# Attention scores in 128 rows, the last MLP pair in plain products, and the last key products in whole fp32, in a two-layer decoder segment

## The chip, the core and the metric

One NeuronCore of a Trainium2 chip runs the whole program in one launch. The metric is the device time of one execution in microseconds, the median of three runs: 1142.87 us (1142.51 to 1142.96) before the change. The engines are TensorE (PE: matrix products and transposes; PEld is its weight load), VectorE (DVE), ScalarE (ACT), GpSimd (POOL) and SyncE (SP, which issues most DMAs). The work of each engine is a list that it goes through in order.

## The reference, cut to what matters

Two layers, each of a mixer (sparse attention, retention, RWKV-7, short convolution), a cross-attention into 256 memory tokens and a squared-ReLU MLP, on 256 tokens of width 1024, all in fp32. The three places that the change touches:

```python
# mixer A: scores of the selected and the windowed branch, 4 heads of 64, here over all 256 keys
s = einsum('bqhd,bkd->bhqk', qb, k) * scale + bias          # then mask, softmax, times values
# cross-attention: keys of the memory tokens, one product per layer
k, v = jnp.split(rms_norm(mem, ln_mem[l]) @ xa_wkv[l], 2, axis=-1)
# MLP, and the norm at the layer's end
h = rms_norm(x, ln_mlp_pre[l])
x = x + rms_norm(jnp.square(jax.nn.relu(h @ mlp_w1[l])) @ mlp_w2[l], ln_mlp_post[l])
# the next layer begins with h = rms_norm(x, ln_mix_pre[l + 1])
```

## The kernel before, in words

**Precision.** A fast product reads fp32r operands. For full precision each operand is split in two fp32r parts, `hi` (ACT copies) and `lo` (DVE subtracts: `split`), and a product becomes three matmuls (`mm3`): hi·hi, hi·lo, lo·hi. A product of unsplit fp32 operands is one `mm`, which the chip's records show as two passes. Tokens stand in two blocks of 128 (`t`), so there are two of each row-wise step.

**Weights** come in units of 128x1024 numbers. `unit_order` lists them; `unit` brings one by DMA into a `raw` tile and splits it into a `hi` and a `lo` tile. `ftile` multiplies a unit of eight 128x128 blocks with the split, transposed activations: 8 x 3 matmuls of 256 columns.

**Order.** All operations are recorded first; `Sched` then deals them out to the engines' lists by estimated start times, with `rank` to break ties (lower goes first). `NB` gives the number of buffers of each tag. Tag `g8` (8 KB in each partition) has 7: each pair of split activations takes 2, and so does each pair of W2 sums in the MLP. PSUM has 8 banks, named by use: A, B, C and S.

**Attention scores** (`nsa_proj`, `nsa_pair`). The queries of two heads lie in rows 0-63 and 64-127 of one tile; the keys are stored twice, once in each half. A score tile is one `mm3` over the 64 rows of its head: 64x256 and 64x512 numbers moving, by token block; 8 such per layer, 16 in all.

**MLP** (`mlp`, `wpair`). Step j of 16: `up(j)` makes two units of W1 products (48 matmuls into one C bank), ReLU and square. `down(j)` multiplies with a pair of W2 units. It uses the seven-product form of a 2x2 block product: `factors` makes seven left sums, `wpair` four right operands and three right sums (the sums `u` and `w` in `g8`; part of it by an accumulating POOL DMA), and the seven `mm3` go into seven S banks, which stay open until j = 15. In layer 0 the order is up(0), then up(j) and down(j-1); in layer 1 up(j) and down(j-2). After the last products `comb` adds banks up to the four output blocks, and `post_bank` and `post` do the norm of a token block: a square with a sum on ACT, two small POOL operations (a scale-and-add and a power) and two DVE updates of `x` (tiles x_65 and x_67 for the blocks).

**Between the layers** `boundary` calls `post` and then `pre`: again squares on ACT and three POOL operations for the next norm, then DVE makes x·rstd·g, PE transposes it (8 per block, to C banks, `to_hT_half`), and ACT and DVE split the result into the next layer's activations. PE meanwhile works on `kpairs(1, (2, 3))`: four of the eight key units of layer 1 (B banks), held back for this place by `s.after`.

**Helpers.** Every record carries the line of its helper: L622 ACT operations, L633 DVE and POOL tensor_tensor, L639 scalar_tensor_tensor, L645 tensor_scalar, L667 the POOL power, L676 matmuls, L681 transposes, L716 DMAs of SP. In the changed kernel these lines are one lower. Numbers at the ends of tile names count the allocations.

Of the kernel before, what the change touches and what calls it, by code (L numbers as in the profile page):

```python
# [20 lines left out]
T = 256  # L21
# [3 lines left out]
C = 64  # L25
# [61 lines left out]
def unit_order():  # L87

    o = []
    for l in range(DEPTH):  # L90
        def add(lay, *names):
            o.extend((lay, n) for n in names)

        add(l, *[("rwkv", i) for i in RWKV_ORDER])
        add(l, ("nq", 0), ("nq", 1), ("kcvc", 0), ("kskw", 0))
        add(l, *[("tok%d" % g, k0) for g in (1, 2) for k0, _ in NT_CHUNKS])
        add(l, *[("ret", i) for i in range(4)])
        add(l, *[("conv", i) for i in range(6)])
        for m in Z_ORDER:
            for c in range(2):  # L100
                add(l, *[("z", m, c, k0) for k0 in range(0, 8, 2)])
                add(l, ("br", m, c))
        add(l, *[("mo", k) for k in range(8)])
        xv = [[("xv", c, k0) for k0 in range(0, 8, 2)] for c in range(2)]
        if l == 0:
            add(l, *[("xk", k) for k in range(8)])
        else:
            add(l, *xv[0])
        add(l, *[("xq", k) for k in range(8)])
        if l == 0:  # L110
            add(l, *xv[0])
        add(l, *xv[1])
        add(l, *[("xo", k) for k in range(8)])
        if l == 0:
            add(1, *[("xk", k) for k in range(4)])
        add(l, *[("w1", i) if l == 0 else ("w1t", 2 * i) for i in range(4 - 2 * (l == 0))])
        lag = 1 if l == 0 else 2
        for j in range(lag, 16 + lag):
            if j < 16:
                add(l, ("w1", 2 * j), ("w1", 2 * j + 1))  # L120
            add(l, ("w2", j - lag, 0), ("w2", j - lag, 1))
        if l == 0:
            add(1, *[("xk", k) for k in range(4, 8)])
    return o
# [105 lines left out]
NPS = {"A": 4, "B": 2, "C": 2, "S": 7}  # L230
# [367 lines left out]
class Prog:  # L598
# [332 lines left out]
    def pre(self, t, g, hT, normed, out):  # L931
# [11 lines left out]

        if normed:
            rstd = stat()
            for s in H2:
                self.stt(xg[:, s], x[:, s], rstd, g[:, s], OP.mult, OP.mult)
        else:
            for s in H2:
                self.tt(xg[:, s], x[:, s], g[:, s], OP.mult)  # L950
        for q in range(2):
            self.to_hT_half(t, q, xg[:, 512 * q:512 * q + 512], hT)
# [432 lines left out]
    def nsa_proj(self, l, hT):  # L1385
# [6 lines left out]
        q2 = pair()  # L1392
        self.split(*q2, q)
# [17 lines left out]
        self.nsap = q, L, q2, k2  # L1411
# [265 lines left out]
    def mem_prep(self, l):  # L1677
# [12 lines left out]
        mh, ml = self.new_hT()  # L1690
        for i in range(0, 8, 2):
            m = self.tile([128, 2, T], "g2")
# [13 lines left out]
    def kpairs(self, l, pairs, spill=None):  # L1706
        for i in pairs:
            p = self.bank("B", (128, 2, T))
            for j in range(2):
                self.ftile(l, ("xk", 2 * i + j), self.mhl, p[:, j])  # L1710
# [21 lines left out]
    def xattn(self, l):  # L1732
# [66 lines left out]
        if l == 0:  # L1799
            self.at(5, self.mem_prep, 1)  # L1800
# [64 lines left out]
    def mlp(self, l):  # L1865
        hT, rstd = self.hT, self.rs
        left = {}

        def factors(j, put):
# [3 lines left out]
            if a is not put:  # L1873
                put(a)
# [10 lines left out]
        def up(j):  # L1885
# [38 lines left out]
        if l == 0:  # L1924
            up(0)
        else:
# [12 lines left out]
        lag = 1 if l == 0 else 2  # L1939
        for j in range(lag, 14 + lag):  # L1940
            if j < 16:
                up(j)
            down((j - lag,), (1, 3, 2, 5, 7, 6, 4))
        if l == 0:
            up(15)
# [7 lines left out]
        down((14,), (1, 2, 6, 5, 3))  # L1953
        down((15,), (1, 2, 6, 5, 3))
        down((14, 15), (7, 4))
        self.lastdown = self.s.mains[-1]
# [3 lines left out]
        def end(t):  # L1960
            if last:
                self.post(t, st[t], rstd[t], out=orr[:, t])
            else:
                self.at(0, self.boundary, t, st[t], rstd[t], gpre, outT, True, self.rs)
# [8 lines left out]
        old = self.rank(0)  # L1973
# [4 lines left out]
        u4 = comb(u2, bank[5], OP.add)  # L1978
        comb(bank[3], u4, OP.subtract, 0, 1)
        end(0)  # L1980
        u3 = comb(u2, bank[7], OP.add)
        comb(u3, bank[5], OP.add, 1, 1)
# [6 lines left out]
    def run(self):  # L1989
# [5 lines left out]
        for l in range(DEPTH):  # L1995
# [72 lines left out]
```

## Time and profile before

| what | value |
|---|---|
| median of 3 runs | 1142.87 us |
| the profiled execution: its time, its span | 1143.17 us, 1141.4 us |
| mean granted TensorE clock | 0.994 |
| read from HBM, written | 223.48 MB, 3.15 MB |
| matmul records on PE | 7380 |

The span is from the first to the last instruction; 1.77 us of the execution lie around it. Windows and timelines count from the span's start. The mixer of layer 0 lies at 10 to about 290 us, its cross-attention up to about 400, its MLP up to 577, the change of layers at 577 to 600, and layer 1 follows in the same way, with its MLP from about 960 to 1130. A record's duration runs to the modelled end of the result; matmuls overlap, so what a matmul costs in a dense stretch is the distance from one start to the next.

### The profile page before, as it was taken

The numbers are of one execution on the slowest core, as the hardware profiler recorded it, in microseconds if no ns is written. First come the engines' busy times: TensorE is split into PE (matmuls) and PEld (weight loads), VectorE is DVE, ScalarE is ACT, GpSimd is POOL, SyncE is SP. The second block draws the span as 40 slices with busy tenths as digits, with TensorE's granted clock in tenths as the row PEclk, the third lists the DMA queues.
The fourth block names the chain that finished last, engine by engine and source line by source line (L and its number), as shares of the span: only waits on it lengthen the run. The fifth ranks groups of instructions, "written<-read, shape, count | busy, mean of one in ns | idle before, by whom it ended". The sixth has DMA issues, their size and how long they took to land. (4 is left out here: it accounts for less than half of the span.)

```text
span 1141.4 us, 19231 instructions
## 1 busy us (share of the span) xinstructions
PE 1113.1 (98%) x7380; PEld 977.0 (86%) x7380; DVE 868.9 (76%) x1332; ACT 662.6 (58%) x1055; POOL 105.3 (9%) x165
## 2 busy tenths in 40 slices
PE   8999999999999999999979999999999999999996
PEld 7898878788998899999869899888888986999994
DVE  5867785675857689989896678766857667998897
ACT  7545544544645567677674546454547455776673
POOL 3002000100200110000021002000002002000011
PEclk9999999999999999999999999999999999999998
DMA  8327456754537599999853155456655467899991
GB/s 323 119 89 242 128 155 194 251 193 148 184 131 240 181 271 277 289 278 257 281 188 106 32 194 171 148 168 192 223 192 167 141 213 211 242 271 280 261 267 52
DMA packets 76831, 226.83 MB, mean 199 GB/s; under 512 B 12319, under 2 KB 14111, under 8 KB 76612
## 3 DMA queue, kind: packets, MB, share of 16 engines
q1 hardware_dynamic: 72132, 208.83, 54.8%
q0 software_dynamic: 4608, 16.78, 8.5%
q8 instruction: 58, 0.95, 0.3%
q14 instruction: 33, 0.27, 0.1%
HBM read 223.48 MB, written 3.15 MB: 199 GB/s over the span
## 5 line engine op out<-in xcount | busy, mean ns | idle before, releaser
L633 DVE TENSOR_TENSOR lo<-raw,hi 128x1024 fp32r<-128x1024 f32 (+2 forms) x310 | 370.1, 1213 | 95.7 <-ACT hi L622 67.5
L622 ACT ACTIVATE hi<-raw 128x1024 fp32r<-128x1024 f32 (+2 forms) x310 | 317.7, 1049 | 139.8 <-PE A L676 83.6
L676 PE MATMUL A<-hi,g 128*128 128x512 f32 (+2 forms) x1152 | 368.1, 391 | 0.8 <-ACT g L622 0.5
L676 PEld LDWEIGHTS A<-hi,g 128*128 128x128 f32 x1152 | 215.0, 188 | 47.6 <-issue 2.2
L676 PE MATMUL A<-lo,g 128*128 128x512 f32 (+2 forms) x576 | 221.4, 384 | 0.0
L633 DVE TENSOR_TENSOR g<-g,g 128x512 f32<-128x512 f32 (+3 forms) x228 | 196.8, 891 | 5.7 <-ACT g L622 4.5
L622 ACT ACTIVATE g<-g 128x512 fp32r<-128x512 f32 (+7 forms) x232 | 155.2, 706 | 62.7 <-DVE g L633 41.2
L676 PE MATMUL A<-g,hi 128*128 128x256 f32 x928 | 179.3, 292 | 1.2 <-DVE g L633 1.2
L676 PE MATMUL C<-g,hi 128*128 128x256 f32 x960 | 172.0, 281 | 0.0
L676 PEld LDWEIGHTS A<-g,hi 128*128 128x128 f32 x928 | 145.1, 191 | 9.6 <-issue 6.3
L676 PEld LDWEIGHTS C<-g,hi 128*128 128x128 f32 x960 | 149.4, 189 | 2.4
L676 PE MATMUL C<-g,lo 128*128 128x256 f32 x480 | 135.1, 281 | 0.0
L676 PE MATMUL A<-g,lo 128*128 128x256 f32 x464 | 131.5, 283 | 0.4 <-DVE lo L633 0.4
L622 ACT ACTIVATE g<-C 128x512 fp32r<-128x512 f32 (+5 forms) x119 | 59.7, 515 | 117.2 <-PE C L676 80.5
L676 PEld LDWEIGHTS A<-lo,g 128*128 128x128 f32 x576 | 108.5, 188 | 20.9 <-issue 0.5
L676 PE MATMUL S<-g,g 128*128 128x512 f32 x480 | 117.1, 394 | 0.0
L676 PEld LDWEIGHTS S<-g,g 128*128 128x128 f32 x480 | 90.1, 188 | 21.0
L676 PEld LDWEIGHTS C<-g,lo 128*128 128x128 f32 x480 | 90.5, 189 | 0.0
L676 PEld LDWEIGHTS A<-g,lo 128*128 128x128 f32 x464 | 88.6, 191 | 0.6 <-DVE lo L633 0.6
L622 ACT ACTIVATE g<-A 128x512 f32<-128x512 f32 (+2 forms) x66 | 37.3, 566 | 54.1 <-PE A L676 51.3
L676 PE MATMUL B<-g,g 64*64 64x64 f32 (+4 forms) x896 | 67.8, 253 | 0.0
L676 PEld LDWEIGHTS B<-g,g 64*64 64x64 f32 (+2 forms) x896 | 59.0, 151 | 6.0 <-issue 2.1
(142 smaller groups left out, 1079.7 us busy)
## 6 DMA issues: line engine op xcount, KB each, us to landing
raw<-wts SPq DMA_DIRECT2D x298, 512.0 KB, 4.6
g<-wts SPq DMA_DIRECT2D x96, 256.0 KB, 5.7
g<-wts POOLq DMA_DIRECT2D x32, 512.0 KB, 6.5
g<-rows SPq DMA_DIRECT2D x11, 512.0 KB, 4.4
g<-memT SPq DMA_DIRECT2D x12, 256.0 KB, 5.9
g<-cmpw SPq DMA_DIRECT2D x4, 512.0 KB, 4.7
raw<-wts SPq DMA_DIRECT2D x4, 498.0 KB, 3.6
raw<-wts SPq DMA_DIRECT2D x4, 480.0 KB, 6.8
```

The costliest lines, as they stand in the source:

```text
L622: e = lambda: self.nc.scalar.activation(real(out), real(in_), func, bias=real(bias), scale=real(scale), accum_out=real(accum))
L633: f = lambda: e.tensor_tensor(real(out), real(a), real(b), op)
L676: e = lambda: self.nc.tensor.matmul(real(out), real(lhsT), real(rhs), start=start, stop=stop, skip_group_check=True)
```

## The change

1. **Scores in 128 rows.** `nsa_proj` now keeps the split queries of one head in one tile `qs`, `hi` in rows 0-63 and `lo` in rows 64-127. A score is two matmuls over 128 rows, with the `hi` and with the `lo` keys, which stand in both halves already. (The sum now has lo·lo as well.)
2. **Close of the MLP, both layers.** Step 15 no longer uses the seven-product form: `whole` and `plain` multiply its four left and right blocks as eight plain `mm3`. Banks 1, 5, 6 and 7 are complete after step 14, and their sums are put ahead at rank -1.5; a bank 8 is opened late. Layer 0 takes the order of layer 1 (down two steps behind up).
3. **Norm between the layers.** `pre` computes x·g at once; the factor rstd enters by the product that transposes, with a scaled identity, in fp32 instead of the transpose.
4. **Last key products.** The four key units held back multiply the unsplit weights with an unsplit, normalised memory tile `mraw` (a `g8` tile that lives from the cross-attention of layer 0 to here), as eight fp32 products each.

```diff
-        add(l, *[("w1", i) if l == 0 else ("w1t", 2 * i) for i in range(4 - 2 * (l == 0))])
-        lag = 1 if l == 0 else 2
-        for j in range(lag, 16 + lag):
+        add(l, *[("w1", i) if l == 0 else ("w1t", 2 * i) for i in range(4)])
+        for j in range(2, 18):
...
-            add(l, ("w2", j - lag, 0), ("w2", j - lag, 1))
+            add(l, ("w2", j - 2, 0), ("w2", j - 2, 1))
...
-    def to_hT_half(self, t, q, src, hT):
+    def to_hT_half(self, t, q, src, hT, scale=None):
...
-            self.tr(p[:, j], src[:, j * 128:(j + 1) * 128])
+            if scale is None:
+                self.tr(p[:, j], src[:, j * 128:(j + 1) * 128])
+            else:
+                self.mm(p[:, j], src[:, j * 128:(j + 1) * 128], scale)
...
+        for s in H2:
+            self.tt(xg[:, s], x[:, s], g[:, s], OP.mult)
+        scale = None
         if normed:
-            rstd = stat()
-            for s in H2:
-                self.stt(xg[:, s], x[:, s], rstd, g[:, s], OP.mult, OP.mult)
...
+            scale = self.tile([128, 128], "g1")
+            self.ts(scale, self.ident, stat())
...
-        q2 = pair()
-        self.split(*q2, q)
+        qs = self.tile([128, 2, 2, T], "g4", F32R)
+        for s in range(2):
+            self.split(qs[0:64, :, s], qs[64:128, :, s], p[64 * s:64 * s + 64])
...
-                self.mm3(p, *[v[po, a, t * 128:t * 128 + 128] for v in q], *[v[po, :, :nk] for v in k], True, True)
+                qt = q[:, a, h % 2, t * 128:t * 128 + 128]
+                with self.together():
+                    self.mm(p, qt, k[0][:, :, :nk], True, False)
+                    self.mm(p, qt, k[1][:, :, :nk], False, True)
...
+    def ftile_whole(self, l, name, moving, dst):
...
+        raw = self.tile([128, UNIT], "raw")
+        d = self.dma(raw, self.wts[i], lead=False)
...
+                for k in (k0, k0 + 1):
+                    self.mm(dst, raw[:, k * 128:(k + 1) * 128], moving[:, k, :], k == 0, k == 7)
...
-                    self.mm3(bank[n], *left[j][n], *right[j][n], j == 0, j == 15)
+                    self.mm3(bank[n], *left[j][n], *right[j][n], j == 0, j == 14 and n not in (2, 3, 4))
...
+        down((14,), (1, 6, 5, 7, 2, 3, 4))
+        old = self.rank(-1.5)
         self.act(p1, bank[1])
-        comb(p1, bank[2], OP.add, 0, 0)
         u2 = comb(p1, bank[6], OP.add)
         u4 = comb(u2, bank[5], OP.add)
+        u3 = comb(u2, bank[7], OP.add)
+        u5 = comb(u3, bank[5], OP.add)
+        self.rank(old)
+        bank[8] = self.bank("S")
+        us = [self.unit(l, ("w2", 15, h)) for h in range(2)]
...
+        plain(2, (0, 0, 0), (1, 1, 0))
+        plain(3, (0, 1, 1), (1, 0, 1))
+        self.rank(-1.5)
+        comb(p1, bank[2], OP.add, 0, 0)
         comb(bank[3], u4, OP.subtract, 0, 1)
         end(0)
+        self.rank(old)
+        plain(8, (3, 1, 1), (2, 0, 1))
+        plain(4, (3, 0, 0), (2, 1, 0))
...
+        comb(u5, bank[8], OP.add, 1, 1)
         comb(bank[4], u3, OP.subtract, 1, 0)
         end(1)
...
-                self.kpairs(1, (2, 3), self.kscr)
+                self.kpairs(1, (2, 3), self.kscr, True)
```

Along PE's list the tile of the array that a matmul uses (its rows by its columns) changes 115 times before and 89 times after the change. Three places show the moves.

On PE in the mixer of layer 0, two score tiles of the second pair of heads (C_1767 and C_1834 before, C_1850 and C_1853 after; A banks are the projections around them). Before:

```order
L676 MATMUL A_1775<-g_4_194,hi_1424 128x256
L676 MATMUL A_1775<-g_3_184,lo_1498 128x256
L676 MATMUL C_1834<-g_193_934,g_182_784 128x512
L676 MATMUL C_1834<-g_194_957,g_182_784 128x512
L676 MATMUL C_1834<-g_193_934,g_183_800 128x512
L676 MATMUL A_1775<-g_3_184,hi_1424 128x256
L676 MATMUL A_1775<-g_4_194,hi_1424 128x256
```

After:

```order
L675 MATMUL A_1842<-hi_1488,g_3_184 128x512
L675 MATMUL A_1842<-lo_1625,g_3_184 128x512
L675 MATMUL A_1842<-hi_1488,g_4_194 128x512
L675 MATMUL C_1850<-g_192_948,g_182_926 128x256
L675 MATMUL C_1850<-g_193_963,g_182_926 128x256
L675 MATMUL C_1853<-g_192_948,g_182_926 128x512
L675 MATMUL C_1853<-g_193_963,g_182_926 128x512
L675 MATMUL A_1842<-hi_1488,g_3_184 128x512
```

Three matmuls over 64 rows became two over 128, and these two tiles now stand next to each other, later among the projections.

On PE at the change of layers (B: key products; C: the 16 transposes; A: first projection of layer 1). Before:

```order
L681 MATMUL C_6479<-ident,g_1200_6464 128x128 x4
L676 MATMUL B_6408<-g_758_3864,hi_6275 128x256
L676 MATMUL B_6408<-g_759_3873,hi_6275 128x256
L676 MATMUL B_6408<-g_758_3864,lo_6296 128x256
...
L681 MATMUL C_6536<-ident,g_1218_6533 128x128 x4
L681 MATMUL C_6545<-ident,g_1218_6533 128x128 x4
L676 MATMUL A_6558<-g_1167_6491,hi_6289 128x256
```

After, from the last MLP product (S_4654, bank 4) on:

```order
L675 MATMUL S_4654<-hi_6201,g_1150_6232 128x512
L675 MATMUL B_6295<-g_759_3790,raw_6144 128x256 x8
L675 MATMUL B_6295<-g_759_3790,raw_6161 128x256 x4
L675 MATMUL C_6346<-g_1196_6337,g_1195_6309 128x128 x4
L675 MATMUL C_6357<-g_1196_6337,g_1195_6309 128x128 x4
L675 MATMUL B_6295<-g_759_3790,raw_6161 128x256 x4
L675 MATMUL B_6381<-g_759_3790,raw_6177 128x256 x8
L675 MATMUL C_6416<-g_1214_6408,g_1213_6384 128x128 x4
L675 MATMUL C_6425<-g_1214_6408,g_1213_6384 128x128 x4
L675 MATMUL B_6381<-g_759_3790,raw_6208 128x256 x8
L675 MATMUL A_6454<-g_1163_6359,hi_6252 128x256
```

Before, 84 of the 96 key matmuls stood ahead of the first transposes; now 12 of the 32 fp32 key products stand ahead of block 0's products with the scaled identity (g_1196), 12 between the two blocks and 8 behind them.

On DVE at the end of layer 1 (S: banks; s: the norm's factor from POOL). Before:

```order
L633 TENSOR_TENSOR g_2355_12111<-g_2354_12107,S_10492 128x512
L639 SCALAR_TENSOR_TENSOR g_2346_12097<-g_2350_12109,g_2322_11878 128x512
L639 SCALAR_TENSOR_TENSOR g_2357_12121<-g_2355_12111,g_2322_11878 128x512
L633 TENSOR_TENSOR g_2359_12125<-S_10510,g_2354_12107 128x512
L639 SCALAR_TENSOR_TENSOR x_65<-g_2346_12097,s_12123,x_65 128x512 x2
L639 SCALAR_TENSOR_TENSOR g_2357_12121<-g_2359_12125,g_2322_11878 128x512
L639 SCALAR_TENSOR_TENSOR x_67<-g_2357_12121,s_12134,x_67 128x512 x2
```

After:

```order
L632 TENSOR_TENSOR g_2336_11985<-S_10374,g_2322_11953 128x512
L638 SCALAR_TENSOR_TENSOR g_2334_11976<-g_2336_11985,g_2309_11774 128x512
L632 TENSOR_TENSOR g_2340_11996<-g_2324_11963,S_11981 128x512
L638 SCALAR_TENSOR_TENSOR g_2342_12005<-g_2340_11996,g_2309_11774 128x512
L638 SCALAR_TENSOR_TENSOR x_65<-g_2334_11976,s_12003,x_65 128x512 x2
L632 TENSOR_TENSOR g_2344_12013<-S_10406,g_2323_11958 128x512
L638 SCALAR_TENSOR_TENSOR g_2342_12005<-g_2344_12013,g_2309_11774 128x512
L638 SCALAR_TENSOR_TENSOR x_67<-g_2342_12005,s_12021,x_67 128x512 x2
```

The update of x_65, which waits for POOL, now stands ahead of the sum of the last bank (S_10510 before, S_10406 after).

More of the change, by code (lines that the diff above doesn't have):

```diff
@@ L1690, in mem_prep @@
         mh, ml = self.new_hT()
+        self.mraw = self.tile([128, 8, T], "g8") if whole else None
         for i in range(0, 8, 2):
-            m = self.tile([128, 2, T], "g2")
+            m = self.mraw[:, i:i + 2] if whole else self.tile([128, 2, T], "g2")
             self.dma(m, self.memT[:, i:i + 2])
@@ L1704, in half, with kpairs @@
         return [self.tile([128, 1024], "g4", F32R).rearrange("p (k m) -> p k m", k=4) for _ in range(2)]
-    def kpairs(self, l, pairs, spill=None):
+    def ftile_whole(self, l, name, moving, dst):
+        i = self.taken
+        assert ORDER[i] == (l, name)
+        self.taken += 1
+        old = self.rank("split")
+        raw = self.tile([128, UNIT], "raw")
+        d = self.dma(raw, self.wts[i], lead=False)
+        d.deps.setdefault(self.lastsplit[0], -9.0)
+        self.lastsplit = (d, *self.lastsplit[1:])
+        self.rank(old)
+        for k0 in range(0, 8, 2):
+            with self.together():
+                for k in (k0, k0 + 1):
+                    self.mm(dst, raw[:, k * 128:(k + 1) * 128], moving[:, k, :], k == 0, k == 7)
+    def kpairs(self, l, pairs, spill=None, whole=False):
         for i in pairs:
@@ L1709, in kpairs @@
             for j in range(2):
-                self.ftile(l, ("xk", 2 * i + j), self.mhl, p[:, j])
+                if whole:
+                    self.ftile_whole(l, ("xk", 2 * i + j), self.mraw, p[:, j])
+                else:
+                    self.ftile(l, ("xk", 2 * i + j), self.mhl, p[:, j])
             if spill is None:
@@ L1867, in mlp, with whole @@
         left = {}
+        def whole(put):
+            a = self.tile([128, 4, 128], "g4")
+            put(a, 3)
+            hl = [self.tile([128, 4, 128], "g2", F32R) for _ in range(2)]
+            self.split(*hl, a)
+            left[15] = [[v[:, i] for v in hl] for i in range(4)]
         def factors(j, put):
@@ L1873, in factors @@
             if a is not put:
[L1874 removed]
+                put(a, 7)
             old = self.rank(1)
@@ L1925, in mlp @@
             up(0)
+            up(1)
         else:
@@ L1936, in down @@
                         right[j] = self.wpair(l, j)
-                    self.mm3(bank[n], *left[j][n], *right[j][n], j == 0, j == 15)
[L1939 to L1945, printed above, removed]
+                    self.mm3(bank[n], *left[j][n], *right[j][n], j == 0, j == 14 and n not in (2, 3, 4))
+        for j in range(2, 16):
+            up(j)
+            down((j - 2,), (1, 3, 2, 5, 7, 6, 4))
         gpost = self.bcast_row(l, "ln_mlp_post")
@@ L1971, in comb, with plain @@
             return c
-        old = self.rank(0)
         p1 = g2()
+        down((14,), (1, 6, 5, 7, 2, 3, 4))
+        old = self.rank(-1.5)
         self.act(p1, bank[1])
-        comb(p1, bank[2], OP.add, 0, 0)
         u2 = comb(p1, bank[6], OP.add)
         u4 = comb(u2, bank[5], OP.add)
+        u3 = comb(u2, bank[7], OP.add)
[3 more added lines that the diff above has]
+        us = [self.unit(l, ("w2", 15, h)) for h in range(2)]
+        def plain(n, *terms):
+            for i, (a, h, c) in enumerate(terms):
+                self.mm3(bank[n], *left[15][a], *[v[:, 512 * c:512 * c + 512] for v in us[h]], n == 8 and i == 0, i == 1)
+        plain(2, (0, 0, 0), (1, 1, 0))
+        plain(3, (0, 1, 1), (1, 0, 1))
+        self.rank(-1.5)
+        comb(p1, bank[2], OP.add, 0, 0)
         comb(bank[3], u4, OP.subtract, 0, 1)
         end(0)
-        u3 = comb(u2, bank[7], OP.add)
-        comb(u3, bank[5], OP.add, 1, 1)
+        self.rank(old)
+        plain(8, (3, 1, 1), (2, 0, 1))
+        plain(4, (3, 0, 0), (2, 1, 0))
+        self.lastdown = self.s.mains[-1]
+        self.rank(-1.5)
+        comb(u5, bank[8], OP.add, 1, 1)
         comb(bank[4], u3, OP.subtract, 1, 0)
```

28 lines of the change are left out of this document (12 added, 16 removed).

## The prediction

> **What bounds the kernel now.** I read the page first, then the list of waits of PE, then windows and timelines of the four places that change.
>
> ```profile
> PE 1113.1 (98%) x7380; PEld 977.0 (86%) x7380; DVE 868.9 (76%) x1332; ACT 662.6 (58%) x1055; POOL 105.3 (9%) x165
> ...
> PE   8999999999999999999979999999999999999996
> ```
>
> PE is busy for 98% of the span, with one dent in the middle (the change of layers) and one at the end. So a matmul less on PE counts in full, as long as the others can follow, and the idle time left lies at a few places:
>
> ```profile
> PE C L681 <- DVE g L639: 6.0, 2, 4.1
> ...
> PE A L676 <- DVE g L633: 1.5, 2, 1.2
> ```
>
> Columns: us in total, times, longest. The 6.0 us before transposes and most of the 1.5 are the change of layers. Whether the others can follow, the windows say (busy time of PE, PEld, DVE, ACT, POOL, then the clock and the DMA share):
>
> ```profile
> 120.00:140.00 20.00, 20.00 (x152) 17.26 (x152) 12.41 (x32) 11.50 (x30) 0.65 (x4) 1.00 0.39 118
> 440.00:460.00 20.00, 20.00 (x135) 18.35 (x134) 18.61 (x25) 14.53 (x18) 1.73 (x2) 1.00 0.93 277
> 720.00:740.00 20.00, 20.00 (x115) 15.05 (x115) 17.36 (x33) 9.58 (x21) 0.39 (x2) 1.00 0.48 139
> ```
>
> Around the scores (120 and 720) DVE and ACT have room; in the MLP (440) DVE has 1.4 of 20 us left.
>
> **1. Scores.** A score tile of 64x256 and one of 64x512 between projections:
>
> ```profile
> 130.92 0.40 PE L676 MATMUL A<-g,hi 128*128 128x256 f32 x2
> 131.15 0.28 PE L676 MATMUL A<-g,lo 128*128 128x256 f32 x1
> 131.36 0.62 PE L676 MATMUL C<-g,g 64*128 64x256 f32 x3
> 131.91 0.50 PE L676 MATMUL A<-g,hi 128*128 128x256 f32 x2
> 132.25 0.28 PE L676 MATMUL A<-g,lo 128*128 128x256 f32 x1
> ...
> 136.59 0.28 PE L676 MATMUL A<-g,lo 128*128 128x256 f32 x1
> 136.79 0.95 PE L676 MATMUL C<-g,g 64*128 64x512 f32 x3
> 137.67 0.50 PE L676 MATMUL A<-g,hi 128*128 128x256 f32 x2
> 138.01 0.28 PE L676 MATMUL A<-g,lo 128*128 128x256 f32 x1
> ...
> 1116.68 3.65 PE L676 MATMUL S<-g,g 128*128 128x512 f32 x15
> 1120.16 0.39 PE L676 MATMUL S<-hi,g 128*128 128x512 f32 x1
> ```
>
> Dense matmuls of 256 columns start 0.23 / 2 = 0.118 us apart (130.92 to 131.15), those of 512 columns (1120.16 - 1116.68) / 15 = 0.232. The 64-row ones are no faster: three take three steps. So one matmul less in each of 16 tiles is 8 x 0.118 + 8 x 0.232 = **-2.8 us**. The visit itself costs more. From 131.15 to 132.25 six matmuls start; at 0.118 they would take 0.71, and it is 1.10. With 512 columns, 136.59 to 138.01 is 1.42 against 3 x 0.118 + 3 x 0.232 = 1.05. So going to 64 rows and back costs 0.37 to 0.39 us beyond the matmuls, about 0.195 for each change of the array's tile. In the new lists the tile changes 89 times instead of 115: -26 x 0.195 = **-5.1 us**. No row shows 128-row score matmuls; if all of the surplus stayed, the term would be 0, and if each visit lost 0.39, -6.2. I take -5.1, since A's matmuls next to A's show no surplus. The queries' split adds one ACT and one DVE operation of 512 columns a layer (0.6 and 0.7 us), off PE's path by the windows; without that cover 2 x 1.3 us.
>
> **2. MLP of layer 0 and the change of layers.** PE before:
>
> ```profile
> 564.44 0.39 PE L676 MATMUL S<-hi,g 128*128 128x512 f32 x1
> ...
> 570.66 0.50 PE L676 MATMUL S<-hi,g 128*128 128x512 f32 x1 [1.23 <-ACT g L622]
> ...
> 572.38 0.50 PE L676 MATMUL S<-hi,g 128*128 128x512 f32 x1 [1.00 <-DVE g L633]
> ...
> 576.90 0.40 PE L676 MATMUL B<-g,hi 128*128 128x256 f32 x2
> ...
> 588.88 0.65 PE L681 MATMUL C<-ident,g 128*128 128x128 f32 x4 [1.86 <-DVE g L639]
> ...
> 595.54 1.97 PE L681 MATMUL C<-ident,g 128*128 128x128 f32 x8 [4.15 <-DVE g L639]
> 597.34 0.58 PE L676 MATMUL A<-g,hi 128*128 128x256 f32 x1
> 599.08 0.58 PE L676 MATMUL A<-g,hi 128*128 128x256 f32 x1 [1.15 <-DVE g L633]
> ...
> 602.21 0.40 PE L676 MATMUL A<-g,hi 128*128 128x256 f32 x2
> ```
>
> *Close.* Steps 14 and 15 are 42 matmuls, 42 x 0.232 = 9.74 us, but last from 564.44 to 576.90, 12.46: 2.7 lost to waits for the sums of steps 14 and 15. Now step 13's 21 matmuls (4.9 us) stand behind the last `up` too, step 15 needs no sums (on DVE two splits of 1024 instead of two adds and splits of 512 and three of 1024), and its 24 plain matmuls are 3 more than 21, +0.7. I take the waits as gone: **-2.0 us** (0 if DVE has fallen behind by then).
>
> *Boundary.* From 576.90 to the first projection. At 602.21 fifteen projection matmuls have run (one at 597.34, fourteen from 599.08); dense they take 15 x 0.118 = 1.8, so PE stands as if it had begun at 600.4: 23.5 us for the stretch. Part of it ran slowly:
>
> ```profile
> 595.00:602.00 7.00, 5.31 (x22) 4.78 (x23) 6.91 (x8) 2.26 (x3) 0.00 (x0) 0.52 0.86 286
> ```
>
> The clock was 0.52 after the gap of 4.15. The new stretch holds 32 key products and 16 with the scaled identity, all fp32:
>
> ```profile
> 23.67 0.38 PE L676 MATMUL B<-g,g 128*128 128x256 f32 x1
> 25.32 1.02 PE L676 MATMUL B<-g,g 128*128 128x256 f32 x4
> ...
> 74.75 1.95 PE L676 MATMUL B<-g,g 128*128 128x128 f32 x16
> ```
>
> An fp32 product is two records. Of 256 columns a record takes (1.02 - 0.38) / 3 = 0.213, so a product 0.43; of 128 columns (1.95 - 0.28) / 15 = 0.111 (0.28 is one such record), a product 0.22. That makes 32 x 0.43 + 16 x 0.22 = 17.3 us without a wait; the old one held 96 x 0.118 + 16 transposes at about 0.11 = 13.1, so PE's work grows by 4.2. Do the factors arrive in time? POOL and DVE before:
>
> ```profile
> 585.38 1.74 POOL L633 TENSOR_TENSOR s<-s 128x1 f32<-128x1 f32 x1 [3.42 <-ACT junk L622]
> 588.07 1.42 DVE L639 SCALAR_TENSOR_TENSOR g<-x,s,g 128x512 f32<-128x512 f32 x2 [1.01 <-POOL s L667]
> 593.24 0.19 POOL L645 TENSOR_SCALAR s<-s 128x1 f32<-128x1 f32 x1
> 593.51 0.55 POOL L667 TENSOR_TENSOR s<-s,mhalf 128x1 f32<-128x1 f32 x1
> ```
>
> Let E be the end of the last MLP product. Block 0's second bank closes 12 matmuls earlier, at E - 2.8. Behind it stand a DVE sum (0.7), the ACT square (0.9 from the sum's end to POOL's start, as from 1133.56 to 1134.48 in part 3), two POOL operations (0.8 to 2), x (1.4), a second square (0.9), three POOL operations (1.3 to 2.5) and the scaled identity (0.2): E + 4.2 to 6.4. PE is done with the first 12 key products at E + 5.2, so it waits 0 to 1.2. Block 1's chain runs behind the same in-order lists of DVE, ACT and POOL and is done at about E + 11 to 13; PE gets there at E + 12.2 or later. The last 8 products (3.4 us) cover the split of block 1. So 17.3 to 18.8; I take 18.2, a gain of 23.5 - 18.2 = **-5.3 us**. The key weights stay raw, which spares DVE and ACT four splits of 1024; `raw` loads behind them find other buffers.
>
> The clock fell behind the gap of 4.15; what a gap of 3 does, no row shows, so the third rival below has two prices. The Trainium skill, "TensorE: Matmul & The Clock Gate", section "What's actually happening", says that it takes an idle window of about 3.4 us to halve the clock; by that rule the lower of the two prices holds up to such a gap and the higher one beyond.
>
> **3. The end.** Layer 1 before, from the last products on:
>
> ```profile
> 1125.88 0.50 PE L676 MATMUL S<-hi,g 128*128 128x512 f32 x1 [0.23 <-DVE g L633]
> ...
> 1132.88 0.68 DVE L633 TENSOR_TENSOR g<-S,g 128x512 f32<-128x512 f32 x1
> 1133.81 1.41 DVE L639 SCALAR_TENSOR_TENSOR x<-g,s,x 128x512 f32<-128x512 f32 x2 [0.25 <-POOL s L667]
> ...
> 1136.59 1.41 DVE L639 SCALAR_TENSOR_TENSOR x<-g,s,x 128x512 f32<-128x512 f32 x2 [0.77 <-POOL s L667]
> ...
> 1134.48 1.42 POOL L645 TENSOR_SCALAR s<-s,s 128x1 f32<-128x1 f32 x1 [0.71 <-ACT junk L622]
> ```
>
> Steps 14 and 15 start at 1120.16; 45 matmuls end at about 1130.6 (three more than before, one wait less). Three of four blocks can now be summed under the plain products; the last, bank 4, at 1130.7. But on DVE the update of x_65 stands ahead of it and waits for POOL: second bank closed 1128.0, sum 1128.7, square 1129.5, POOL until 1130.5 to 1131.2, x_65 until 1132 to 1132.6. Then bank 4's sum, square and POOL: if that POOL operation takes 1.42 again, x_67 starts at 1136.3, 0.3 earlier than 1136.59; if 0.2 to 0.5, at 1134.4 to 1135.3. In the old run it took 1.42 while DVE wrote x, and 0.19 at 593.24; now DVE is idle there. I take **-1.5 us** (0 to -2.2).
>
> The Trainium skill, "SBUF — State Buffer", section "SBUF: two separate sides", says that a DVE operation with two SBUF inputs locks out a GpSimd one that reads SBUF. By that rule the gain would be 1.3 to 2.2; the 1.74 at 585.38 beside DVE's splits agrees, and no run here shows the new order.
>
> **Sum.** -5.1 - 2.8 - 2.0 - 5.3 - 1.5 = -16.7. The profiled execution took 1143.17 with a span of 1141.4, 0.3 over the median; 1143.17 - 16.7 - 0.3 = **1126.2 us** against 1142.87.
>
> **Rivals.** *The cost of a visit stays*: it belongs to the small products, not to 64 rows. Then only the score matmuls go: -16.7 + 5.1, 1131.3. For it: no row of the new kind. Against: 0.37 to 0.39 with 256 and 512 columns alike. 12%.
> *PE's time saved at the scores comes back as waits*: half of 7.9 returns, 1130.2. For it: DVE at 17.36 of 20 at 720. Against: PE never waits between 90 and 220. 8%.
> *The norms arrive late*: DVE's and POOL's lists delay block 0 or 1 by 3 to 4 us more; about 1129.7; if that gap brings the slow clock back for 3 us of work, 1131. For it: six POOL operations that took up to 1.74. Against: DVE has four splits less. 14%.
> *Slower: `mraw` leaves W2's sums two `g8` buffers in layer 0* instead of three, so a pair's sums can be split only when PE has let go of the last pair's. The chain from there is 1.1 (ACT) and 1.2 (DVE), 2.5 us with the hand-overs; PE meanwhile has 48 x 0.118 and five of seven products, 9.1 us. With DVE at 18.61 of 20, the two splits may queue behind other work. The change is slower than before once each of 14 pairs waits more than 16.7 / 14 = 1.2 us; at 2 us it is 1154. Layer 1's MLP, in the same order with more room, shows no such wait. 5%.
>
> **How the numbers follow.** The forecast has 61%, its own range 1123 to 1129. The range 1122 to 1132.5 leaves out the slow rival and sums of two others. A measurement tells about 0.2% (2.3 us) from no change. Faster 0.93 (the forecast and three rivals), same 0.02, slower 0.05.
>
> **What would show it.** Scores: no 64x256 triples, A's starts 0.12 apart around C, PE's counts 16 fewer there. Boundary: B to A in 17 to 19 us, clock at 1.0, no wait over 1.5. Close of layer 0: 66 S matmuls without a wait. End: x_67 no later than 1119 in the new span, a POOL operation under 0.6 before it. It would be wrong if PE waited in layer 0's MLP, or if the starts around the new score tiles kept a surplus of 0.2.

## The result, and the profile after

The changed kernel takes 1125.52 us (median of four runs, 1124.35 to 1126.79) against 1142.91 for the kernel before on the same chips: a ratio of 0.9848 with a 95% interval of 0.9831 to 0.9865. That is 17.4 us less; the forecast was 16.7 less, 1126.2. The profiled execution took 1125.16 us with a span of 1123.4, 18.0 shorter than the span before. In one experiment below, the small sums on DVE, one of four runs took 2773.89 us and is left out.

The page of the changed kernel, busy times and the row of slices for PE:

```profile
PE 1107.5 (99%) x7354; PEld 976.4 (87%) x7354; DVE 857.0 (76%) x1318; ACT 653.2 (58%) x1049; POOL 98.8 (9%) x163
...
PE   9999999999999999999999999999999999999996
```

PE has lost its dent in the middle; the dent at the end stays. The list of PE's waits (total, times, longest) has none over 1.4 us:

```profile
PE C L675 <- DVE g L644: 1.4, 1, 1.4
...
PE C L680 <- DVE g L632: 1.0, 1, 1.0
PE C L675 <- ACT g L621: 0.5, 1, 0.5
```

The first of them (1.4 us) is the wait for block 1's scaled identity at the change of layers, the second lies in layer 1's cross-attention, where the kernel before had it too, and the third lies ahead of the second step of layer 0's MLP. The kernel before has none there, but with the changed kernel's list up to there it took from 0 to 1.06 us in the executions below.

Where the 18 us came from, by stages between starts of the same PE records in the two profiled executions (the first projection of layer 1 is reckoned back from dense records, as in the prediction):

| stage, up to | before | after | difference |
|---|---|---|---|
| the last wide projection of layer 0's mixer | 286.77 | 281.75 | -5.0 |
| the last wide projection of its cross-attention | 106.21 | 105.02 | -1.2 |
| its last MLP product | 183.69 | 184.02 | +0.3 |
| the first projection of layer 1 | 23.7 | 19.3 | -4.4 |
| the last wide projection of layer 1's mixer | 271.5 | 267.0 | -4.5 |
| the last wide projection of its cross-attention | 99.19 | 98.11 | -1.1 |
| its last MLP product | 159.09 | 159.31 | +0.2 |
| the end of the span | 11.26 | 8.90 | -2.4 |

Each column is one execution. A second one of the changed kernel (below) has 282.07 in the first row, 183.38 in the third, and the others within 0.1.

PE's timeline of the changed kernel at the places of the prediction: a pair of score tiles, one step of W1 products in layer 0, the close of that MLP, the change of layers, and the last product:

```profile
135.23 0.39 PE L675 MATMUL A<-hi,g 128*128 128x512 f32 x1
135.46 0.86 PE L675 MATMUL C<-g,g 128*128 128x256 f32 x4
136.15 0.39 PE L675 MATMUL A<-hi,g 128*128 128x512 f32 x1
...
443.75 0.40 PE L675 MATMUL C<-g,hi 128*128 128x256 f32 x2
...
448.43 0.40 PE L675 MATMUL C<-g,hi 128*128 128x256 f32 x2
...
555.37 0.39 PE L675 MATMUL S<-hi,g 128*128 128x512 f32 x1
...
570.79 0.40 PE L675 MATMUL S<-hi,g 128*128 128x512 f32 x1
571.03 5.34 PE L675 MATMUL B<-g,raw 128*128 128x256 f32 x24
576.21 1.95 PE L675 MATMUL C<-g,g 128*128 128x128 f32 x16
577.99 5.35 PE L675 MATMUL B<-g,raw 128*128 128x256 f32 x24
584.71 2.05 PE L675 MATMUL C<-g,g 128*128 128x128 f32 x16 [1.37 <-DVE g L644]
586.60 3.62 PE L675 MATMUL B<-g,raw 128*128 128x256 f32 x16
589.86 0.58 PE L675 MATMUL A<-g,hi 128*128 128x256 f32 x2
...
1114.50 0.39 PE L675 MATMUL S<-hi,g 128*128 128x512 f32 x1
```

Four score matmuls over 128 rows (two of 256 and two of 512 columns) take 136.15 - 135.46 = 0.69 us; 2 x 0.118 + 2 x 0.232 is 0.70, so **the surplus of a visit is gone**. The close, 66 S matmuls, lasts 571.03 - 555.37 = 15.66, and 66 x 0.232 is 15.3: no wait. The change of layers, from 571.03 to a dense start at 590.05, takes 19.0, and the clock (third number from the end) is 1.00 where it was 0.52 before:

```profile
585.00:592.00 7.00, 7.00 (x49) 6.59 (x49) 6.62 (x8) 4.82 (x6) 0.37 (x1) 1.00 0.97 354
```

DVE and POOL there and at the end, in two fences:

```profile
584.37 0.29 DVE L644 TENSOR_SCALAR g<-ident,s 128x128 f32<-128x128 f32 x1 [0.72 <-POOL s L666]
...
1114.86 1.40 DVE L638 SCALAR_TENSOR_TENSOR x<-g,s,x 128x512 f32<-128x512 f32 x2
1116.18 0.68 DVE L632 TENSOR_TENSOR g<-S,g 128x512 f32<-128x512 f32 x1
...
1118.84 1.42 DVE L638 SCALAR_TENSOR_TENSOR x<-g,s,x 128x512 f32<-128x512 f32 x2 [1.25 <-POOL s L666]
```

```profile
576.55 1.47 POOL L644 TENSOR_SCALAR s<-s,s 128x1 f32<-128x1 f32 x1 [0.84 <-ACT junk L621]
...
581.90 0.66 POOL L632 TENSOR_TENSOR s<-s 128x1 f32<-128x1 f32 x1 [3.24 <-ACT junk L621]
582.66 1.04 POOL L644 TENSOR_SCALAR s<-s 128x1 f32<-128x1 f32 x1
...
1117.79 0.37 POOL L644 TENSOR_SCALAR s<-s,s 128x1 f32<-128x1 f32 x1 [3.02 <-ACT junk L621]
```

x_67 starts at 1118.84, 4.3 us behind the last product (1114.50); before it was 6.45 behind. POOL's operation ahead of it took 0.37.

### The profile page after: what moved, and what is told of

The parts are those of the page before. It is cut to its first block, busy times and chain, and to the rows that moved or that the text cites. A ratio compares the mean times of both kernels' runs of the same rounds, so it can differ in the third digit from the quotient of the medians.

```text
span 1123.4 us, 19170 instructions
## 1 busy us (share of the span) xinstructions
PE 1107.5 (99%) x7354; PEld 976.4 (87%) x7354; DVE 857.0 (76%) x1318; ACT 653.2 (58%) x1049; POOL 98.8 (9%) x163
## 4 chain that ended last, share of the span: by engine, by line
PE 72%; DVE 3%; DMA 2%; ACT 2%; POOL 1%; issue 1%; POOLq 0%; DVEq 0%; SPq 0%; ACTq 0%
PE A L675 34%; PE C L675 17%; PE S L675 12%; PE B L675 8%; DMA g<-wts 2%; PE C L680 2%; DVE g L632 1%; ACT junk L621 1%; ACT g L621 1%; POOL s L644 1%; DVE x L638 0%; POOL s L666 0%; ACT hi L621 0%; DVE lo L632 0%; PE B L680 0%
## 5 line engine op out<-in xcount | busy, mean ns | idle before, releaser
L632 DVE TENSOR_TENSOR lo<-raw,hi 128x1024 fp32r<-128x1024 f32 (+1 forms) x308 | 368.7, 1213 | 99.3 <-ACT hi L621 73.4
L621 ACT ACTIVATE hi<-raw 128x1024 fp32r<-128x1024 f32 (+1 forms) x308 | 316.4, 1049 | 121.0 <-PE A L675 70.4
L632 DVE TENSOR_TENSOR g<-g,g 128x512 f32<-128x512 f32 (+3 forms) x218 | 188.2, 887 | 10.1 <-ACT g L621 8.8
L621 ACT ACTIVATE g<-g 128x1024 fp32r<-128x1024 f32 (+7 forms) x224 | 147.6, 698 | 49.5 <-DVE g L632 23.8
L621 ACT ACTIVATE g<-C 128x512 fp32r<-128x512 f32 (+4 forms) x119 | 59.4, 515 | 127.3 <-PE C L675 100.8
L675 PE MATMUL S<-g,g 128*128 128x512 f32 x450 | 109.8, 394 | 0.1
L675 PEld LDWEIGHTS S<-g,g 128*128 128x128 f32 x450 | 84.4, 188 | 20.3 <-DVE g L632 0.5
L621 ACT ACTIVATE g<-A 128x512 f32<-128x512 f32 (+3 forms) x70 | 39.8, 569 | 60.7 <-PE A L675 59.3
```

The lines of the kernel that those rows point to most:

```text
L621: e = lambda: self.nc.scalar.activation(real(out), real(in_), func, bias=real(bias), scale=real(scale), accum_out=real(accum))
L632: f = lambda: e.tensor_tensor(real(out), real(a), real(b), op)
L675: e = lambda: self.nc.tensor.matmul(real(out), real(lhsT), real(rhs), start=start, stop=stop, skip_group_check=True)
```

## The experiments

Each was timed beside the kernel before on the same chip; the ratios to it have 95% intervals. The changed kernel's ratio is 0.9848.

### Scores: rows or number of matmuls?

*The kernel before with part 1 alone:*

```
-        q2 = pair()
-        self.split(*q2, q)
+        qs = self.tile([128, 2, 2, T], "g4", F32R)
+        for s in range(2):
+            self.split(qs[0:64, :, s], qs[64:128, :, s], p[64 * s:64 * s + 64])
...
-                self.mm3(p, *[v[po, a, t * 128:t * 128 + 128] for v in q], *[v[po, :, :nk] for v in k], True, True)
+                self.mm(p, qt, k[0][:, :, :nk], True, False)
+                self.mm(p, qt, k[1][:, :, :nk], False, True)
```

> The kernel before with part 1 alone (scores in 128 rows). 16 matmuls fewer and 88 tile changes instead of 115. My theory, that a change of tile costs 0.195 us: -2.8 - 27 x 0.195 = -8.1, so 1134.8 us, and no surplus around the score tiles in the trace. The rival that a visit costs the same whatever its rows: -2.8, so 1140.1. The rival that half returns as waits: 1138.9.

*Two matmuls as well, but over the 64 rows of before* (hi·hi and hi·lo of the old `q2`):

> The kernel before with two matmuls in each score tile, still over 64 rows; the product of the queries' lo part with the keys' hi part is left out. 16 matmuls fewer, 111 tile changes instead of 115. My theory: -2.8 - 4 x 0.195 = -3.6, so 1139.3, and each visit keeps its surplus of 0.37 to 0.39 us, so it stays 4.5 behind scores in 128 rows. The rival that the surplus belongs to small products and not to the rows: the same time as scores in 128 rows alone, whatever that is.

Measured: 1136.53 us, ratio 0.9944 (0.9932 to 0.9957), that is -6.4 us, for 128 rows; 1140.08, 0.9973 (0.9964 to 0.9982), -3.1 us, for two matmuls in 64 rows. The difference, 3.3 us, comes with the rows and with the order of the list that goes with them. PE's timeline of the 64-row kernel:

```profile
135.54 0.28 PE L676 MATMUL A<-g,lo 128*128 128x256 f32 x1
135.75 0.51 PE L676 MATMUL C<-g,g 64*128 64x256 f32 x2
136.18 0.50 PE L676 MATMUL A<-hi,g 128*128 128x512 f32 x1
136.52 0.39 PE L676 MATMUL A<-lo,g 128*128 128x512 f32 x1
```

From 135.54 to 136.52 run three matmuls of 256 columns and one of 512, 3 x 0.118 + 0.232 = 0.59, in 0.98: the surplus of 0.39 is there with two matmuls as with three. So the rival that the cost belongs to small products has fallen. Of the 8.1 expected of 128 rows, 1.7 did not come. The profiled execution took 1138.25 and won 4.9. In it layer 0's mixer lost 3.0 us, but the stretch from layer 0's last product to the end of layer 1's mixer only 0.4. The change of layers, which this edit does not touch, looks so on PE and in the windows of the 128-row kernel:

```profile
591.85 1.97 PE L681 MATMUL C<-ident,g 128*128 128x128 f32 x8 [5.86 <-DVE g L639]
...
595.38 0.58 PE L676 MATMUL A<-g,hi 128*128 128x256 f32 x1 [1.15 <-DVE g L633]
```

```profile
590.00:597.00 7.00, 4.00 (x16) 3.47 (x17) 6.29 (x9) 1.48 (x3) 0.92 (x2) 0.58 0.89 286
597.00:604.00 7.00, 7.00 (x45) 7.00 (x44) 2.90 (x4) 2.33 (x5) 2.09 (x4) 0.69 0.47 155
```

Block 0's transposes come without a wait now, and block 1's behind a gap of 5.86 us (1.86 and 4.15 before). PE's waits there are no longer than before in all: 5.86 + 1.15 against 1.86 + 4.15 + 1.15. But the clock is then halved for 10.24 us instead of 6.83, and for another 3.41 us at 10.88, behind a wait of 2.10 us in the first projections. PE is busy throughout both of these 3.41 us, and half of that is 1.7: 3.4 us in all, about the 3.2 that this execution lacks of the 8.1. By this estimate they were lost to the clock, and not to waits that the scores made. In the changed kernel the gap is gone.

### Layer 0's MLP: why did 2 us not come?

The change was to win 2.0 us there; it lost 0.3 in the first execution and won 0.3 in the second. The waits in the close are gone, but W1 matmuls start 119.3 ns apart on the mean of the whole MLP, where before it was 117.8: over some 760 of them 1.1 us; and 0.5 us is waited at the second step.

*The order of before, the new close kept* (with the units' order to match):

```
-            up(1)
...
-        for j in range(2, 16):
+        lag = 1 if l == 0 else 2
+        for j in range(lag, 14 + lag):
             up(j)
-            down((j - 2,), (1, 3, 2, 5, 7, 6, 4))
+            down((j - lag,), (1, 3, 2, 5, 7, 6, 4))
+        if l == 0:
+            up(15)
```

> The changed kernel with the order of before in layer 0's MLP: W2 products one step behind W1 products instead of two, the new close kept. The traces show W1 matmuls 0.1194 us apart in layer 0 after the change and 0.1178 before it, W2 matmuls 0.2333 and 0.2316, and one wait of 0.5 us ahead of the second step. Theory A, that the order of steps sets this pace: 0.1178 and 0.2316 come back and the wait goes, 760 x 0.0016 + 325 x 0.0017 + 0.5 = 2.3 us less, 1123.2. Theory B, that the pace comes from the two W2 buffers that the memory tile leaves, or from elsewhere: no change, 1125.5.

Measured: 1125.9 us, 0.9849 (0.9836 to 0.9863), W1 matmuls 119.3 ns apart. PE at the close:

```profile
560.58 0.39 PE L679 MATMUL S<-hi,g 128*128 128x512 f32 x1
...
570.79 0.40 PE L679 MATMUL S<-hi,g 128*128 128x512 f32 x1
```

Here the last 45 S matmuls stand together; 44 of them start within 570.79 - 560.58 = 10.21 us, and 44 x 0.232 is 10.21. So the new close has no waits one step behind either. Layer 0's MLP takes 182.7 us instead of 184.0: the wait at the second step is gone, and so is 0.36 us that the close of the first execution took beyond its matmuls. But five executions with the changed kernel's list and buffers there took 182.8 to 184.0, so what the order itself costs is not shown. The pace is not back: **the order is not its cause**, my first theory fell, and the total shows no gain. The kernel with split keys (below) has no memory tile, and there the pace is 118.0. That leaves the number of `g8` buffers for W2's sums or the place of the operands. (The number is four in the changed kernel, and three before and with split keys: the whole memory tile takes one, but the split one lets go of its two early on. The prediction, and the expectation below, count two in the changed kernel; that is wrong.)

*Same lists, other buffers:* in the choice of a free slot,

```
+                w = {'g8_719': 0, 'g8_720': 4, 'g8_759': 2, 'g8_762': 1, 'g8_763': 3}.get("_".join(t.name.split("_")[:2]), i)
+                i = w if f[w] is not None else i
```

The activations are g8_762 and g8_763. The other three tiles named keep the buffers that they had; W2's sums take what is left, still four.

> The changed kernel, every engine's list the same, but the split activations of layer 0's MLP lie in the g8 buffers in which the kernel before and the one with split keys have them (second and fourth of seven, instead of fourth and fifth); the memory tile, and with it the number of buffers for the W2 sums, stays. W1 matmuls were 118.0 ns apart in both of those and 119.2 in the changed kernel and in the one with one step. Theory A, that the place of the operands sets the pace: 118.0 in layer 0, 760 x 1.2 ns = 0.9 us less, 1124.6. Theory B, that the two buffers that are left for the W2 sums set it: 119.2 stays, 1125.5.

Its W1 products of one step, on PE:

```profile
446.06 0.40 PE L677 MATMUL C<-g,hi 128*128 128x256 f32 x2
...
449.59 0.39 PE L677 MATMUL C<-g,hi 128*128 128x256 f32 x2
```

Thirty matmuls start in 449.59 - 446.06 = 3.53 us, 117.7 ns each; in the changed kernel's rows above, 39 in 448.43 - 443.75 = 4.68, 120 ns. On the mean of layer 0's MLP it is 117.9 against 119.3, and W2 matmuls go from 231.9 to 232.3. **So the place sets this pace**, theory A: that of the moving operand, or of W2's sums, which changes with it. The total, 1125.43 us at 0.9837 (0.9819 to 0.9856), does not tell the gain; the stage takes 183.3 instead of 184.0, and not 1.1 less, since the wait at the second step was 1.06 this time.

### The close: what is it worth, and where?

*The changed kernel with the old close in both layers* (`factors` for step 15 too, `down` of 14 and 15 in the old order, the sums behind it):

```
-        down((14,), (1, 6, 5, 7, 2, 3, 4))
...
+        down((14,), (1, 2, 6, 5, 3))
+        down((15,), (1, 2, 6, 5, 3))
+        down((14, 15), (7, 4))
```

> The changed kernel with the old close of the MLP in both layers (seven-product form for the last pair, sums behind it); the order two steps behind stays in layer 0. My theory: the waits for the sums of the last two steps return in layer 0 (2.7 - 0.7 = 2.0 us), block 0's norm begins up to 2.8 us later at the change of layers (0 to 2 us of waits), and the end gets 1.5 to 2.4 us longer: 1129 to 1132. The rival, that two steps of distance alone take the waits away: only the end, 1127 to 1128.

Measured: 1132.78 us, 0.9907 (0.9893 to 0.9922), 7.3 us slower than the changed kernel. But not where I had put it. PE, from the close of layer 0 to layer 1, and windows of 1 us behind the gap:

```profile
557.47 0.39 PE L675 MATMUL S<-hi,g 128*128 128x512 f32 x1
...
572.29 1.02 PE L675 MATMUL B<-g,raw 128*128 128x256 f32 x4
```

```profile
584.00 2.05 PE L675 MATMUL C<-g,g 128*128 128x128 f32 x16 [0.32 <-DVE g L644]
585.88 2.76 PE L675 MATMUL B<-g,raw 128*128 128x256 f32 x12
590.73 3.54 PE L675 MATMUL C<-g,g 128*128 128x128 f32 x16 [2.09 <-DVE g L644]
593.92 0.56 PE L675 MATMUL A<-g,hi 128*128 128x256 f32 x1
```

```profile
589.00:590.00 1.00, 0.00 (x0) 0.00 (x0) 1.00 (x2) 1.00 (x3) 0.63 (x2) 1.00 0.98 401
...
592.00:593.00 1.00, 1.00 (x7) 1.00 (x6) 1.00 (x2) 0.85 (x2) 0.00 (x0) 0.50 1.26 154
```

Its 63 S matmuls take 572.29 - 557.47 = 14.8 us, 63 x 0.232 = 14.6: the old close has **no waits either**, once `down` runs two steps behind. Either half of the change takes them away: the distance here, the new close in the kernel one step behind. In layer 0's MLP the plain products are even a loss of their three matmuls, 0.7 us. What they pay is behind it. Block 0's products with the scaled identity come 11.7 us behind the first key product (584.00) instead of 5.2 (576.21), block 1's 18.4 (590.73) instead of 13.7; PE waits 2.09 there and then runs at half clock for 3.41 us. From the last product to the end of layer 1's mixer this kernel takes 4.9 us more, and its end 11.25 instead of 8.90, 2.35 more: 7.3 together. Its two MLPs took 1.8 less, and layer 0's mixer, which the edit leaves alone, 2.7 more in this execution, so that 5 to 7 us are the close's.

### The change of layers: the keys and the factor

*Split keys for the four units held back* (`kpairs` and `mem_prep` without the new argument):

> The changed kernel with the last key products split as before (96 fp32r matmuls instead of 32 fp32 products), so no raw memory tile and three W2 buffers in layer 0. At the change of layers PE has 96 x 0.118 + 16 x 0.22 = 14.8 us of work instead of 17.3, and DVE four splits of 1.2 us more ahead of the factor of block 1, which came 13.3 us after the last MLP product. Theory: that stretch takes 16.5 to 19.5 us instead of 19.0, about 1 us less in all if the pace of layer 0's MLP stays (theory A of the order of steps), 1124.5. Theory B (the buffers set the pace): another 1.8 us less, 1122.7. The rival, that the freed splits are what made the stretch short: 2 us or more slower, 1127.5, with waits for the factors of over 3 us.

Measured: 1128.51 us, 0.9873 (0.9858 to 0.9888), 3.0 slower. PE and SP behind the last transposes:

```profile
589.69 0.39 PE L675 MATMUL A<-g,hi 128*128 128x256 f32 x1 [1.65 <-DVE g L632]
...
599.77 2.83 PE L675 MATMUL B<-g,g 128*128 128x256 f32 x12 [2.82 <-DMA g<-lora]
```

```profile
586.37 8.95 SPq L715 DMA_DIRECT2D raw<-wts  x6
595.41 0.37 SPq L715 DMA_DIRECT2D g<-lora  x1
```

The stretch itself got shorter, as its PE work says: the first projection starts 16.0 us behind the first key product (587.66 - 571.67), and with the wait of 1.65 dense work starts at 17.9 instead of 19.0. But the split weights hold buffers, layer 1's weights are issued late, SP reaches the `lora` load behind six of them at 595.41, and PE waits 2.82 for it. So the time is near the rival's, but not for its reason: whole keys cost PE 1 us in the stretch and win 3.7 behind it, in layer 1's mixer (267.0 against 270.7). The pace of layer 0's W1 matmuls, 118.0, is theory B's figure, but its cause turned out to be the place (above).

*The old norm* (`stt` with the factor, transposes; the scaled identity gone):

> The changed kernel with the old norm between the layers (DVE multiplies by the factor, PE transposes). PE's work there falls by 16 x 0.11 = 1.8 us, but block 1's 1.4 us of DVE updates stand behind its factor instead of 0.3 of scaled identity, so its transposes start at 14.7 instead of 13.6 us behind the last MLP product. Theory: the two nearly cancel, the stretch stays within 1 us of 19.0, 1125.5. The rival, that the factor's place is worth much of the gain at the change of layers: 3 us slower, 1128.5.

Measured: 1126.3 us, 0.9852 (0.9838 to 0.9867); the stretch takes 18.4. It nearly cancels, as expected: the scaled identity by itself is worth nothing that can be told.

*The small sums and scalings of the factor on DVE*, the power left on POOL, and at the end the updates of x_65 behind the last sum (as in the next part):

```
-        self.ts(v, acc[:, 0:1], acc[:, 1:2], eps, OP.add, OP.add, pool=True)
+        self.ts(v, acc[:, 0:1], acc[:, 1:2], eps, OP.add, OP.add, pool=not self.dvefac)
```

> The changed kernel with the small sums and scalings of the norm's factor (not the power) on DVE instead of POOL, at the change of layers and at the end, and the updates of x_65 behind the last sum at the end. At the change of layers POOL's operations of 1.47, 0.66 and 1.04 us beside DVE's work become 0.2 each, so block 1's factor comes about 2 us earlier and PE's wait of 1.37 for it goes: -1.4. At the end x_67 starts 3.9 us behind the last product instead of 4.3: -0.4. Theory: 1123.7 against 1125.5 of the changed kernel. The rival, that DVE's list is the limit and the small operations queue behind its splits of 1.2 us: the wait stays over 1 us, 1125 to 1126.

Measured: 1126.6 us, 0.9858 (0.9838 to 0.9877). No gain in all: the end takes 8.36 us instead of 8.90, as expected, but the change of layers 0.7 more. POOL there:

```profile
571.64 0.56 POOL L666 TENSOR_TENSOR s<-s,mhalf 128x1 f32<-128x1 f32 x1 [21.37 <-DVE s L644]
577.83 1.46 POOL L666 TENSOR_TENSOR s<-s,mhalf 128x1 f32<-128x1 f32 x1 [5.63 <-DVE s L644]
579.94 1.40 POOL L666 TENSOR_TENSOR s<-s,mhalf 128x1 f32<-128x1 f32 x1 [0.65 <-DVE s L644]
586.60 1.39 POOL L666 TENSOR_TENSOR s<-s,mhalf 128x1 f32<-128x1 f32 x1 [5.26 <-DVE s L644]
```

The power, 0.56 us in the first row, takes 1.4 where DVE starts a split of 1.22 us just ahead of it (577.67 for the one at 577.83): the time moved from one POOL operation to the next. PE still waits 1.08 for block 1's factor. The rival was right in size, though the reason is as much POOL as DVE's list.

### The end

*The updates of x_65 behind the last bank's sum*, by a dependence that leads to no wait:

```
+            for o in upd:
+                o.deps.setdefault(lastyg, 0.0)
         end(1)
```

> The changed kernel with one thing moved in DVE's list at the end: the two updates of x_65 go behind the last bank's sum and its product with the weights. So ACT's square can start 1.3 us earlier, and POOL's scale-and-add for x_67 then runs beside DVE's updates of x_65. Theory A, that DVE's writes of x hold POOL up: that operation takes 1.2 to 1.5 us instead of 0.37, and x_67 starts 0.2 to 0.4 us earlier behind the last product than the 4.3 of the changed kernel. Theory B, that the 1.42 before had another cause: 0.4 us, and x_67 starts 1.1 us earlier. Total 1124.4 to 1125.2.

Measured: 1124.72 us, 0.9837 (0.9821 to 0.9852). POOL:

```profile
1115.55 1.29 POOL L644 TENSOR_SCALAR s<-s,s 128x1 f32<-128x1 f32 x1 [1.78 <-ACT junk L621]
```

It takes 1.29 beside DVE's updates (1115.27 to 1116.68), against 0.37, and x_67 starts 1117.52 - 1113.51 = 4.0 us behind the last product, 0.3 earlier than in the changed kernel. Theory A; the total alone would not tell 0.3 us. **The Trainium skill**, "SBUF — State Buffer", section "SBUF: two separate sides", says that a DVE operation with two SBUF inputs locks a GpSimd one that reads SBUF out for its whole length; these rows agree with it.

### Together, and once more

*The small sums on DVE, with both MLPs' operands in the second and fourth buffers:*

> The kernel of the small sums on DVE, and besides the split activations of both MLPs in the second and fourth g8 buffers. Theory, that the place of these operands sets the pace of W1 matmuls: about 118 ns apart in both layers (119.2 in layer 0 and 118.9 in layer 1 of the changed kernel), 0.9 us less in layer 0 and 0.6 in layer 1: 1.5 less than with the small sums alone, 1122.2 in all. The rival, that what lies in the other buffers counts as much: 118 in layer 0 and 119 in layer 1, 0.9 less.

Measured: 1123.89 us, 0.9835 (0.9820 to 0.9850), W1 matmuls 117.9 and 117.8 ns apart: the place works in both layers. Here the two activation tiles of each MLP are the only ones named.

*The changed kernel again:*

> The changed kernel once more, beside the two others: 1125.5 (1124.3 to 1126.8), and the ratio to the kernel before 0.985. The first profile had PE wait only 0.27 us for the first projections at 10 us, where the kernels of the experiments with the same first lists showed 2.0; if that differs from execution to execution, this profile shows one of the two, and the kernel's times spread by about that much.

Measured: 1125.49 us, 0.9848 (0.9834 to 0.9863). PE waited 0.80 at 10 us this time, between the 0.27 of the first profile and the 2.00 of the kernel with the old norm, whose lists are the same up to there. Twelve executions with PE's list the same up to there ended layer 0's mixer between 281.0 and 284.4 us, 282.9 on the mean. Five of them waited 1.99 to 2.21 us at 10 us, and then had the clock halved for 3.41 us (see the last section). So 1.2 of the 5.0 us in the first row of the table of stages is chance, and the before column, one execution, has its own.

*What paid, together* (buffers of both layers, and the end):

> The two changes that paid, together, on the changed kernel: the split activations of both MLPs in the second and fourth g8 buffers, and at the end the updates of x_65 behind the last bank's sum; the small sums stay on POOL. W1 matmuls 117.7 to 117.9 ns apart in both layers (760 x 1.3 ns + 690 x 1.2 ns = 1.8 us less), W2 matmuls some 0.4 ns slower (640 x 0.4 ns = 0.3 more), x_67 0.3 us earlier: 1.8 us less than 1125.5, 1123.7. The rival, that the single gains lie within the spread from execution to execution: 1125.5 and no pace below 118.5.

Measured: **1121.62 us** (1121.24 to 1122.81), 0.9815 (0.9802 to 0.9828), W1 matmuls 117.9 and 117.7 apart: faster than both kernels, 3.9 us below the changed one, where 1.8 was expected. Against the first execution of that one layer 0's MLP gave 1.5 (0.9 against the second), layer 1's 0.9, the end 0.3 and layer 1's cross-attention 0.8, which I had not expected and cannot explain; the rest is spread.

## Why the prediction was right, and where not

**Scores (-7.9).** The mechanism is shown: no surplus around 128-row tiles, 0.39 with two matmuls in 64 rows. The size stands within its bounds: -6.4 alone (-4.9 to -7.8, so just short of -7.9). In the changed kernel both mixers lost 9.5, of which 1.2 is chance. The two cross-attentions lost 1.2 and 1.1 that I had no term for. In the kernel with scores alone they lost 0.7 and 1.2, so it comes with the order that this part brings; 0.4 of layer 0's is a wait at 352 us that is gone, and 1.0 of layer 1's two waits of 0.28 and 0.68 at 924 and 954 us. What the rest of layer 0's is stays open.

**Close of layer 0 (-2.0).** The term itself held: the 2.7 us of waits went and 0.7 of matmuls came. What failed is that the term stood for the whole stage, which measured +0.3 in the first execution and -0.3 in the second. The sum put at nothing that the memory tile, by living longer, moves the activations to buffers with slower W1 matmuls (760 x 1.4 ns = 1.1 us), and that the second step can wait: 0.5 in the first execution, 0 to 1.06 in others, behind an ACT copy out of a C bank that ends at 422.45. Another 0.4 the close of the first execution took beyond its matmuls. By the prediction's own sign (wrong if PE waits in layer 0's MLP) that wait counts, small as it is. I had looked at `mraw` only as a taker of buffers, the slower rival; that PE waits for W2's sums did not happen, and they have one buffer more than before, not one less.

**Change of layers (-5.3).** It was -4.4: 19.0 us instead of 18.2. The terms given for block 0 add up to E + 3.4 to 5.8, not to the 4.2 to 6.4 of the text; its scaled identity was ready at E + 5.0, and PE did not wait. Block 1's factor came 13.3 us behind the last product, just past the 11 to 13 of the sum, since POOL's operations took 1.47, 0.66 and 1.04, and PE waited 1.37. The clock stayed at 1.0. What makes it short is the early close: with the old close, gap and slow clock return, and the stage takes 22.7 instead of 19.3. The whole keys help less through PE's cover than behind it, where split keys bring the late `lora` load.

**End (-1.5).** With the MLP's +0.2 it was -2.2, the far bound. POOL's operation took 0.37 with DVE idle beside it, and x_65 did not wait for POOL at all (its factor was ready at 1114.76), so only its own 1.4 us stood ahead of the last sum.

**The sum** came out within 1 us by luck: errors cancelled. In the profiled executions scores and cross-attentions gave 4 more than reckoned, the MLP and the change of layers 3 less.

## What to carry to other kernels

Look for what an early close releases behind it before crediting it with the waits inside it: here the old close was no slower in its own stage, and the new one won 5 to 7 us in the two chains that start at it. When a tile is given a longer life, check not only how many buffers it leaves but where the others' operands land: the same W1 matmuls ran 1% slower. A small POOL operation on the critical chain should stand where DVE has no two-input work; moving it to DVE exposed the next one at the change of layers.

## What the runs showed of the hardware

- **The place of tiles in SBUF sets PE's pace.** fp32r matmuls of 256 columns start 117.7 to 118.0 ns apart with the activations' two parts in the second and fourth `g8` buffers, 118.8 to 119.4 with the seven other pairs that ran, in either layer. The Trainium skill, "SBUF — State Buffer", section "SBUF: two separate sides", says that PE never waits for another engine at its ports; why the place matters no run here shows.
- **The clock can halve after a short gap, and where the gap falls decides.** With the old close, 2.09 us without matmuls were followed by 0.50 in the windows; with split keys a gap of 2.82 us was not, nor the 1.37 of the changed kernel. In all fourteen traces, up to PE's last product, each stretch of one clock that begins and ends in the trace lasts a whole multiple of 3.413 us (3.41, 6.83, 10.24, ...), so the clock changes on a grid. At full clock, every step of this grid in which PE had no matmul running for 1.99 us or more in all was followed by half clock, and none with up to 1.90 was. The 2.09 lay in one step, 587.61 to 591.02; the 2.82 was parted by the step at 598.05, into 1.10 and 1.72. The Trainium skill, "TensorE: Matmul & The Clock Gate", section "What's actually happening", says that the clock falls after an idle window of about 3.4 us, on a window that runs freely; the length of the window agrees, but it need not be idle throughout, and the measurement decides. So both prices of my third rival can come true, by where the gap lies; by an estimate from these figures (2 x 1.90) no gap over 3.8 us escapes.
